# Dilated attention stage of a two-layer encoder: the step without projections between two head groups is taken out

## The chip, the cores and the metric

The kernel runs on one core of a Trainium2 chip. A core has five engines with a queue of instructions each: TensorE (PE, matrix products; its weight loads are listed as PEld), VectorE (DVE), ScalarE (ACT), GpSimd (POOL) and SyncE (SP, which here issues most of the DMAs). An engine takes its queue in order; what it needs of another engine or of a DMA it awaits by semaphore, and everything behind the waiting instruction waits too. Matrix products land in PSUM, of which this stage uses eight banks. The metric is the time of one execution on the device in microseconds (us): the median of the runs.

## What is computed

Two encoder layers over a sequence of 1024 positions with 1024 channels: layer 0 is latent attention, layer 1 is dilated window attention, and each is followed by a squared-ReLU MLP. The change lies in the dilated attention of layer 1, cut here to what matters:

```python
DIL_GROUPS = ((128, 1), (512, 4), (2048, 16))      # (window, dilation)

def dilated_mixer(h, pos, w_in, g_q, g_k, rel_bias, w_o):
    proj = (h @ w_in).reshape(B, S, N_DIL_GROUPS, 3, DIL_HEADS, DIL_HEAD_DIM)
    for gi, (window, dilation) in enumerate(DIL_GROUPS):
        q = rms_norm(proj[:, :, gi, 0], g_q[gi])
        k = rms_norm(proj[:, :, gi, 1], g_k[gi])
        v = proj[:, :, gi, 2]
        o, lse = dilated_group(q, k, v, pos, table, window, dilation)
    wts = jax.nn.softmax(jnp.stack(lses, axis=0), axis=0)
    o = jnp.einsum('gbsh,gbshd->bshd', wts, o_all)
    return o.reshape(B, S, DIL_HEADS * DIL_HEAD_DIM) @ w_o
```

In `dilated_group` the positions are sorted by residue (`_to_residues`), a query sees the keys of its window within its residue, a bias from a table is added, and softmax and the product with v follow. The products are made from float32 split in a high and a low part (three matmuls for one).

## The kernel before

The stage is `dil`. It goes through the three groups one after the other. A group has 16 heads in 8 pairs (`pr`), and a pair takes four steps (`tp` 0 to 3) of two tiles of 128 positions each, so a group has 32 steps. `steps` lists them all. Before the change it has one entry `None` behind each of the first two groups: a step in which PE makes no projections. PE's order is that in which the steps are written (it is pinned from `mark` on); on the other engines a planner places the instructions, so they can stand steps away from where they are written.

One step of the main loop, in PE's order:

- `products` (L1880): score products `pss` of the two tiles that became ready in the step before, from `kT`, six matmuls a tile; a third part of them needs the low half of `kT`, which DVE writes (L1860).
- `project` (L425, L426, L427 in `mm3`): q and k of one tile of 128 positions, 24 matmuls `psproj` from the input tiles `h` in the order d = 0 to 7, each with a high and a low part.
- `stacks` (L1855): four transposes `psq` of the normalized q and k (`qn`) of two steps ago; ACT (L1859) and DVE (L1860) then write `kT`.
- `project` again, for the second tile.
- `av` (L1948, L1949): products of the transposed weights `pT` with v for the tiles whose scores were made in the step before; eight matmuls a tile in the groups 0 and 1, four in group 2. DVE adds the parts up into `U` (L1950).

Beside that `scores` loads the bias `bt` (SP), adds it on DVE (L1894), exponentiates on ACT (L1898, L1900); `attend` splits the weights into `ph` (high part on ACT L1934, low part on DVE or POOL L1935), and a DMA transpose on SP's queue makes `pT` of it (L1936). `qkstep` (L1839 to L1846) normalizes the projections on ACT, DVE and POOL. `v_load` and `v_parts` bring v for two pairs at a time (`vraw` by SP's queue; parts on ACT L1826, DVE L1827, POOL L1828 and L1829). The weights of a pair come as `wqkr` (SP's queue, ACT's for group 2) and are split into `wqkh` on ACT (L121) and `wqkl` on DVE (L122).

The next group needs the same input in another order of positions. `permute(g, dp, k)` copies it: `dp` is a quarter of the channels (d = 2 dp and 2 dp + 1), `k` the high or low part; one call makes two tiles `hTp` by four copies for group 1 and by eight for group 2. The copies go round among the engines: of five, two are on ACT (L2106), two on DVE (L2108), one on POOL (L2110). So there are 32 copies of 128x512 before group 1 and 64 of 128x256 before group 2. The old input has 16 tiles of the pool `gran` with 29 places, and the new needs 16 more, so most of the new tiles take places that something else must leave first. Before the change two of the eight calls are written in the last step of a group and six in the `None` step.

In groups 0 and 1 tile 7 of a pair becomes ready one step later than tiles 5 and 6 (`carry`) and is worked together with tile 0 of the next pair. With the `None` step between, tile 7 of the last pair has an `attend` of its own.

Of the kernel before, what the change touches and what calls it, by code (L numbers as in the profile page):

```python
# [14 lines left out]
AF = mybir.ActivationFunctionType  # L15
ALU = mybir.AluOpType
# [4 lines left out]
P = 128  # L21
# [20 lines left out]
class K:  # L42
# [1717 lines left out]
    def dil(self, at0, at1, tail, wqk, vd):  # L1760
# [147 lines left out]

        def attend(pairs, pe):

            pss = [PS("pss") for _ in range(2)]
            for i, (u, t) in enumerate(pairs):
                products(u, t, pss, i)
            n = len(pairs)
            g = pairs[0][0]["g"]
            m = 4 * P * (1 if g == 2 else 2)
            flat = lambda x: x.rearrange("p i c -> p (i c)")[:, 0 : n * m]
            parts = lambda x: flat(x).rearrange("p (i k c) -> p i k c", i=n, k=2)
            if pe:
                pT = D_("pT", (P, 2, 8 * P), F16, 2)  # L1920
                ps = PS("pspt")
                for i, (u, t) in enumerate(pairs):
                    p = scores(u, t, pss, i)
                    for e in range(2):
                        nc.tensor.transpose(ps[:, (2 * i + e) * P : (2 * i + e + 1) * P], p[:, e], self.ident)
                x = ps[:, 0 : n * 2 * P].rearrange("p (i c) -> p i c", i=n)
                nc.scalar.activation(parts(pT)[:, :, 0], x, AF.Copy)
                nc.vector.tensor_tensor(parts(pT)[:, :, 1], x, parts(pT)[:, :, 0], op=ALU.subtract)
            else:
                ph, pT = (D_(x, (P, 2, 8 * P), F16, 2) for x in ("ph", "pT"))  # L1930
                for i, (u, t) in enumerate(pairs):
                    p = scores(u, t, pss, i)
                    hi, lo = (parts(ph)[:, i, k].rearrange("p (h c) -> p h c", h=2) for k in range(2))
                    nc.scalar.activation(hi, p, AF.Copy)  # L1934
                    (nc.gpsimd if i or g == 2 else nc.vector).tensor_tensor(lo, p, hi, op=ALU.subtract)  # L1935
                nc.sync.dma_start_transpose(out=flat(pT).rearrange("p (b q) -> p b q", q=P), in_=flat(ph))  # L1936
            return [(u, t, parts(pT)[:, i]) for i, (u, t) in enumerate(pairs)]

        def av(u, t, pT):
            g, pr = u["g"], u["pr"]  # L1940
# [115 lines left out]

        steps = []
        for g in range(3):
            steps += [("qk", g, pr, tp) for pr in range(8) for tp in range(4)] + [None] * (1 if g < 2 else 6)
        loads, wts = {}, {}  # L2060
        mark = len(nc.cur_bb.bb.instructions)
        end = max(n for n, x in enumerate(steps) if x is not None)
# [12 lines left out]
        for n, (_, g, pr, _) in firsts.items():  # L2075
            if pr % 2 == 0:
                VS = VSs[(g, pr // 2)] = {}
                VS["load"] = lambda g=g, c=pr // 2, VS=VS: VS.update(raws=v_load(g, c))
                vtodo.setdefault(n - 4, []).append(VS["load"])
                for t in range(0, 9 if g < 2 else 8, 2):  # L2080
                    vtodo.setdefault(n - 2 + t // 2, []).append(lambda t=t, VS=VS: v_parts(VS["raws"], VS, t))
                vtodo.setdefault(n - 2 + t // 2, []).append(lambda VS=VS: VS.pop("raws"))

        h = [at0, at1]
        HT = [at0.tiles, at1.tiles]
# [36 lines left out]
        for n, step in enumerate(steps):  # L2122
            fetch(n + 2)
            for f in vtodo.pop(n, ()):
                f()
            if step is None and perms:
                while perms:
                    permute(*perms.pop(0))
                HT = new
                h = [(lambda k, d, t=t: t[k][d // 2][:, d % 2, :]) for t in HT]  # L2130
            if step is not None and n + 1 < len(steps) and steps[n + 1] is None and step[1] < 2:
                new = [[[], []], [[], []]]
                perms = [(step[1] + 1, dp, k) for dp in range(4) for k in range(2)]
# [226 lines left out]
```

## Time and profile before

| what | value |
| --- | --- |
| median of 3 runs | 3260.46 us (3258.18 to 3262.77) |
| the profiled execution, its own time | 3266.25 us |
| its span | 3264.5 us |
| its granted TensorE clock, mean | 0.982 |
| PE busy | 3145.6 us (96%) |
| dilated stage, first to last projection from `hT` and `hTp` | 1670.9 to 2525.4 us |
| the two places between groups | near 1940 us and 2235 us |

How to read what follows: times are microseconds from the start of the span. A row of the timeline gives start, length, engine, line, what is written and from what, and how many instructions were merged; behind it in brackets, where the engine was idle, how long and what ended the idle time. A row of the view by windows gives the stretch, its length, then for PE, PEld, DVE, ACT and POOL the busy time with the number of instructions, then the granted TensorE clock as a share of full speed, the busy share of the DMA engines, and GB/s. A row of a tile or line gives count and least, median and greatest length in nanoseconds.

### The profile page before, as it was taken

Reading aid. Unit: us, or ns where it says so; the run is one execution under the profiler, and the core shown is the slowest. Engines: PE = TensorE matmul, PEld = TensorE weight load, DVE = VectorE, ACT = ScalarE, POOL = GpSimd, SP = SyncE. Lnnn points to the kernel's source line nnn. Section 1 sums busy time; section 2 is a strip of 40 time slices with the busy share of each in tenths; the row PEclk is TensorE's granted clock in tenths of the full one; section 3 lists DMA queues with packets and bytes.
Section 4 is the critical chain, followed back from the end, with each engine's and each line's share of the span. In section 5 each row is a group of like instructions: output and inputs, shape, how many; then the busy total and the mean of one; then the engine's idle time right before and its main releaser. Section 6 shows DMA issues by size and latency. Waiting matters only on the chain.

```text
span 3264.5 us, 50798 instructions
## 1 busy us (share of the span) xinstructions
PE 3145.6 (96%) x18034; PEld 2660.3 (81%) x18034; DVE 2404.1 (74%) x4272; ACT 1735.4 (53%) x3507; POOL 892.6 (27%) x1197
## 2 busy tenths in 40 slices
PE   6989999999999999999999989998998999999999
PEld 6877677778888788778889989998998788888887
DVE  5677777756977866688767776777888688678566
ACT  5547787754554433542237676666555264444342
POOL 7465555530111000001124444444333002110010
PEclk9999999999999999999999999998999999999999
DMA  5352332252655788535658777887767635439554
GB/s 191 120 188 85 101 95 85 66 188 84 207 184 171 278 228 301 164 126 193 207 142 176 176 176 167 185 181 158 174 153 187 186 104 200 160 138 322 201 192 129
DMA packets 538990, 552.31 MB, mean 169 GB/s; under 512 B 199493, under 2 KB 421106, under 8 KB 538730
## 3 DMA queue, kind: packets, MB, share of 16 engines
q1 hardware_dynamic: 484042, 434.61, 46.8%
q0 software_dynamic: 27360, 91.31, 7.5%
q10 hardware_dynamic: 27328, 23.07, 2.7%
q8 instruction: 144, 2.36, 0.3%
q14 instruction: 116, 0.95, 0.1%
HBM read 376.17 MB, written 132.62 MB: 156 GB/s over the span
## 4 chain that ended last, share of the span: by engine, by line
PE 48%; DVE 5%; DMA 5%; issue 2%; POOL 1%; ACT 1%; SPq 0%; ACTq 0%; DVEq 0%; POOLq 0%
PE psm L426 7%; PE psm L427 7%; PE psm L425 7%; PE psproj L425 4%; PE psproj L426 4%; PE psproj L427 4%; PE pss L1880 2%; DMA pT<-ph 2%; PE psv L426 2%; PE psv L427 2%; PE psv L425 2%; PE psav L1948 1%; PE psy L425 1%; PE psy L427 1%; PE psy L426 1%
## 5 line engine op out<-in xcount | busy, mean ns | idle before, releaser
L426 PE MATMUL psm<-dl,dh 128*128 128x512 f32 x896 | 351.9, 393 | 7.3 <-DVE dl L122 7.2
L425 PE MATMUL psm<-hf,wf 128*128 128x512 f32 x896 | 350.2, 391 | 2.6 <-ACT wf L121 2.6
L427 PE MATMUL psm<-dh,dl 128*128 128x512 f32 x896 | 350.9, 392 | 0.0
L426 PE MATMUL psm<-hf,wf 128*128 128x512 f32 x896 | 349.2, 390 | 0.0
L427 PE MATMUL psm<-hf,wf 128*128 128x512 f32 x896 | 347.3, 390 | 0.4 <-DVE wf L122 0.4
L425 PE MATMUL psm<-dh,dh 128*128 128x512 f32 x896 | 336.5, 393 | 4.9 <-ACT dh L121 4.9
L425 PE MATMUL psproj<-wqkh,hTp 128*128 128x256 f32 x1024 | 307.4, 300 | 0.0
L426 PE MATMUL psproj<-wqkl,hTp 128*128 128x256 f32 x1024 | 294.8, 288 | 0.0
L427 PE MATMUL psproj<-wqkh,hTp 128*128 128x256 f32 x1024 | 294.5, 288 | 0.0
L121 ACT ACTIVATE dh<-ufr 128x1024 fp32r<-128x1024 f32 x112 | 118.3, 1057 | 176.2 <-PE psm L427 52.0
L425 PEld LDWEIGHTS psproj<-wqkh,hTp 128*128 128x128 f32 x1024 | 201.9, 197 | 9.3 <-issue 1.6
L426 PEld LDWEIGHTS psm<-dl,dh 128*128 128x128 f32 x896 | 169.6, 189 | 45.3 <-DVE dl L122 10.1
L425 PEld LDWEIGHTS psm<-dh,dh 128*128 128x128 f32 x896 | 169.0, 189 | 42.3 <-ACT dh L121 7.2
L426 PEld LDWEIGHTS psproj<-wqkl,hTp 128*128 128x128 f32 x1024 | 202.1, 197 | 0.0
L427 PEld LDWEIGHTS psproj<-wqkh,hTp 128*128 128x128 f32 x1024 | 201.3, 197 | 0.0
L425 PEld LDWEIGHTS psm<-hf,wf 128*128 128x128 f32 x896 | 168.6, 188 | 39.8 <-ACT wf L121 5.5
L427 PEld LDWEIGHTS psm<-dh,dl 128*128 128x128 f32 x896 | 169.7, 189 | 35.3
L427 PEld LDWEIGHTS psm<-hf,wf 128*128 128x128 f32 x896 | 168.5, 188 | 36.4 <-DVE wf L122 1.1
L426 PEld LDWEIGHTS psm<-hf,wf 128*128 128x128 f32 x896 | 168.6, 188 | 34.8
L1846 POOL TENSOR_TENSOR qn<-qn,dgain 128x256 f32<-128x256 f32 x96 | 92.1, 959 | 382.1 <-DVE qn L1844 303.0
L122 DVE TENSOR_TENSOR dl<-ufr,dh 128x1024 fp32r<-128x1024 f32 x112 | 136.9, 1222 | 77.2 <-ACT dh L121 58.5
L756 DVE TENSOR_REDUCE mx<-pmx 128x1 f32<-128x512 f32 x256 | 165.1, 682 | 27.5 <-PE pmx L754 27.3
(399 smaller groups left out, 8979.1 us busy)
## 6 DMA issues: line engine op xcount, KB each, us to landing
ufr<-uf SPq DMA_DIRECT2D x112, 512.0 KB
adaw<-in_ada_w SPq DMA_DIRECT2D x96, 512.0 KB
w2r<-in_mlp_w SPq DMA_DIRECT2D x96, 512.0 KB
w1r<-in_mlp_w SPq DMA_DIRECT2D x64, 512.0 KB
bt<-bias SPq DMA_DIRECT2D x128, 256.0 KB
qkv<-st SPq DMA_DIRECT2D x32, 512.0 KB
hraw<-qkv SPq DMA_DIRECT2D x32, 512.0 KB
uf<-ub POOLq DMA_DIRECT2D x32, 512.0 KB, 3.9
```

What stands on the lines that cost most here:

```text
L121: nc.scalar.activation(hi, src, AF.Copy)
L122: (lo_eng or nc.vector).tensor_tensor(lo, src, hi.bitcast(F32), op=ALU.subtract)
L425: mm(out, lh, rh, start=first, stop=False)
L426: mm(out, lh, rl, start=False, stop=False)
L427: mm(out, ll, rh, start=False, stop=last)
L756: nc.vector.tensor_reduce(maxes[h][:, 2 * j + b : 2 * j + b + 1], ps, op=ALU.max, axis=AX.X)
L1846: nc.gpsimd.tensor_tensor(qq, qq, gain[:, g : g + 1, :].unsqueeze(1).broadcast_to([P, 2, 2, 64]), op=ALU.mult)
L1880: nc.tensor.matmul(pss[e][:, i * 256 : (i + 1) * 256], q[r, a, :], u["k"][r, b, w0 : w0 + 256], start=n == 0, stop=n == 2)
L1948: nc.tensor.matmul(o, pT[:, 0, c], v, start=b == 0, stop=False)
```

## The change

The `None` entries behind groups 0 and 1 go; the six at the end of the stage stay. What was written in that step finds other places:

- one `permute` call is written in step `tp` 2 of the group's last pair, two in `tp` 3, and the other five at the head of the next group's first step, ahead of its projections on the other engines' queues;
- tile 7 of a group's last pair is worked with the next group's first tiles: one pair of tiles from two groups between groups 0 and 1, and three tiles together between groups 1 and 2 (group 2 has tiles 0 and 1 ready at once). `attend` therefore takes tiles of different groups and up to three, two score banks for every two tiles; the three fill `ph` and `pT` exactly (2048 columns);
- the first v load of groups 1 and 2 and its parts are written three steps later, counted from the group's first step.

```diff
         def attend(pairs, pe):
-            pss = [PS("pss") for _ in range(2)]
+            pss = []
             for i, (u, t) in enumerate(pairs):
-                products(u, t, pss, i)
-            n = len(pairs)
-            g = pairs[0][0]["g"]
-            m = 4 * P * (1 if g == 2 else 2)
-            flat = lambda x: x.rearrange("p i c -> p (i c)")[:, 0 : n * m]
+                if i % 2 == 0:
+                    pss.append([PS("pss") for _ in range(2)])
+                products(u, t, pss[i // 2], i % 2)
+            m = [4 * P * (1 if u["g"] == 2 else 2) for u, _ in pairs]
+            end = [sum(m[: i + 1]) for i in range(len(m))]
+            flat = lambda x: x.rearrange("p i c -> p (i c)")[:, 0 : end[-1]]
...
-                    (nc.gpsimd if i or g == 2 else nc.vector).tensor_tensor(lo, p, hi, op=ALU.subtract)
+                    (nc.gpsimd if i or u["g"] == 2 else nc.vector).tensor_tensor(lo, p, hi, op=ALU.subtract)
...
-            steps += [("qk", g, pr, tp) for pr in range(8) for tp in range(4)] + [None] * (1 if g < 2 else 6)
+            steps += [("qk", g, pr, tp) for pr in range(8) for tp in range(4)] + [None] * (6 if g == 2 else 0)
...
-                vtodo.setdefault(n - 4, []).append(VS["load"])
+                late = 3 if pr == 0 and g else 0
+                vtodo.setdefault(n - 4 + late, []).append(VS["load"])
                 for t in range(0, 9 if g < 2 else 8, 2):
-                    vtodo.setdefault(n - 2 + t // 2, []).append(lambda t=t, VS=VS: v_parts(VS["raws"], VS, t))
+                    vtodo.setdefault(n - 2 + late + t // 2, []).append(lambda t=t, VS=VS: v_parts(VS["raws"], VS, t))
...
-            if step is None and perms:
+            if step is not None and step[2:] == (0, 0) and perms:
                 while perms:
                     permute(*perms.pop(0))
                 HT = new
                 h = [(lambda k, d, t=t: t[k][d // 2][:, d % 2, :]) for t in HT]
-            if step is not None and n + 1 < len(steps) and steps[n + 1] is None and step[1] < 2:
-                new = [[[], []], [[], []]]
-                perms = [(step[1] + 1, dp, k) for dp in range(4) for k in range(2)]
-                for _ in range(2):
+            if step is not None and step[1] < 2 and step[2] == 7 and step[3] >= 2:
+                if step[3] == 2:
+                    new = [[[], []], [[], []]]
+                    perms = [(step[1] + 1, dp, k) for dp in range(4) for k in range(2)]
+                for _ in range(step[3] - 1):
                     permute(*perms.pop(0))
```

What this makes of PE's order, at the place between groups 0 and 1: before, behind the score products of the `None` step, stand its transposes, its products with v, the next step's score products, and then the first projection from the copied input (`hTp`).

```order
L1880 MATMUL pss_25191<-kT_24580 128x256
L1880 MATMUL pss_25192<-kT_24580 128x256
L1855 MATMUL psq_25230<-ident,qn_24982 128x128 x4
L1948 LDWEIGHTS pT_25024
L1948 MATMUL psav_25237<-vs_24162,pT_25024 128x192
...
L1880 MATMUL pss_25266<-kT_24580 128x256
L1880 MATMUL pss_25267<-kT_24580 128x256
...
L425 MATMUL psproj_25305<-wqkh_25183,hTp_24997 128x256
```

With the change, the same score products are followed at once by the projections of the next group's first step; one of their tiles for d = 2 and 3 (`hTp_25149`) is among those that are copied late.

```order
L1880 MATMUL pss_25181<-kT_24580 128x256
L1880 MATMUL pss_25182<-kT_24580 128x256
L425 MATMUL psproj_25220<-wqkh_25009,hTp_24849 128x256
L426 MATMUL psproj_25220<-wqkl_25010,hTp_24849 128x256
L427 MATMUL psproj_25220<-wqkh_25009,hTp_24997 128x256
...
L425 MATMUL psproj_25220<-wqkh_25009,hTp_25003 128x256
L426 MATMUL psproj_25220<-wqkl_25010,hTp_25003 128x256
L427 MATMUL psproj_25220<-wqkh_25009,hTp_25149 128x256
```

So the transposes, the products with v and one set of score products that stood between two groups' projections now stand behind the next group's first projections.

DVE's queue at the same place, with the change, from the write of `kT` for the next group's first score products to the last copy that the first projection needs (`hTp_25173`, d = 6 and 7, low part). Left out are the four bias additions in the middle, which stand together:

```order
L1860 TENSOR_TENSOR kT_24580<-psq_25083,kT_24580 128x2x256
L122 TENSOR_TENSOR wqkl_25010<-wqkr_24843,wqkh_25009 128x1024
L1953 TENSOR_REDUCE U_24030<-psav_25114 128x128
L1840 TENSOR_REDUCE dms_25135<-dsq_25134 128x8
L1953 TENSOR_REDUCE U_24030<-psav_25124 128x128
L122 TENSOR_TENSOR wqkl_25014<-wqkr_24846,wqkh_25013 128x1024
L2112 CAST hTp_25149<-hTl_20785 128x4x128
L2112 CAST hTp_25155<-hT_3860_18891 128x4x128
L2112 CAST hTp_25158<-hT_3860_18891 128x4x128
...
L2112 CAST hTp_25161<-hsl_19484 128x4x128
...
L2112 CAST hTp_25173<-hT_3880_18987 128x4x128
```

Ten of the 32 copies stand a step or more ahead of this place on their engines; of DVE's 13 copies four do, and the others stand as shown.

On SP's queue three steps ahead of the group's end, before: the v load, then a bias, half of the next weights, and the transpose for the products with v.

```order
L1936 DMA_TRANSPOSE pT_24597<-ph_24596 128x16x128
L1966 DMA U<-U_23473 128x8x128
L1805 DMA vraw_24713<-v 64x256
...
L1810 DMA vraw_24715<-v 64x256
L1889 ISA
L1889 DMA bt_24882<-bias_135 128x2x256
L1562 DMA wqkr_24985<-in_dil_w_in 128x4x128 x2
L1936 DMA_TRANSPOSE pT_24740<-ph_24739 128x16x128
L1562 DMA wqkr_24988<-in_dil_w_in 128x4x128 x2
```

With the change both halves of the weights stand ahead of the v load, and the transpose behind all of it:

```order
L1939 DMA_TRANSPOSE pT_24597<-ph_24596 128x16x128
L1969 DMA U<-U_23473 128x8x128
L1562 DMA wqkr_24843<-in_dil_w_in 128x4x128 x2
L1562 DMA wqkr_24846<-in_dil_w_in 128x4x128 x2
L1889 ISA
L1889 DMA bt_24882<-bias_135 128x2x256
L1805 DMA vraw_24985<-v 64x256
...
L1810 DMA vraw_24987<-v 64x256
L1939 DMA_TRANSPOSE pT_24728<-ph_24727 128x16x128
```

The transpose has moved past two more weight loads of its queue; the v load itself is issued in the same step as before.

More of the change, by code (lines that the diff above doesn't have):

```diff
@@ L1909, in attend @@
         def attend(pairs, pe):
-            pss = [PS("pss") for _ in range(2)]
+            pss = []
             for i, (u, t) in enumerate(pairs):
-                products(u, t, pss, i)
-            n = len(pairs)
-            g = pairs[0][0]["g"]
-            m = 4 * P * (1 if g == 2 else 2)
-            flat = lambda x: x.rearrange("p i c -> p (i c)")[:, 0 : n * m]
-            parts = lambda x: flat(x).rearrange("p (i k c) -> p i k c", i=n, k=2)
+                if i % 2 == 0:
[4 more added lines that the diff above has]
+            flat = lambda x: x.rearrange("p i c -> p (i c)")[:, 0 : end[-1]]
+            parts = lambda x, i: flat(x)[:, end[i] - m[i] : end[i]].rearrange("p (k c) -> p k c", k=2)
             if pe:
@@ L1922, in attend @@
                 for i, (u, t) in enumerate(pairs):
-                    p = scores(u, t, pss, i)
+                    p = scores(u, t, pss[i // 2], i % 2)
                     for e in range(2):
                         nc.tensor.transpose(ps[:, (2 * i + e) * P : (2 * i + e + 1) * P], p[:, e], self.ident)
+                n = len(pairs)
                 x = ps[:, 0 : n * 2 * P].rearrange("p (i c) -> p i c", i=n)
-                nc.scalar.activation(parts(pT)[:, :, 0], x, AF.Copy)
-                nc.vector.tensor_tensor(parts(pT)[:, :, 1], x, parts(pT)[:, :, 0], op=ALU.subtract)
+                y = flat(pT).rearrange("p (i k c) -> p i k c", i=n, k=2)
+                nc.scalar.activation(y[:, :, 0], x, AF.Copy)
+                nc.vector.tensor_tensor(y[:, :, 1], x, y[:, :, 0], op=ALU.subtract)
             else:
@@ L1931, in attend @@
                 for i, (u, t) in enumerate(pairs):
-                    p = scores(u, t, pss, i)
-                    hi, lo = (parts(ph)[:, i, k].rearrange("p (h c) -> p h c", h=2) for k in range(2))
+                    p = scores(u, t, pss[i // 2], i % 2)
+                    hi, lo = (parts(ph, i)[:, k].rearrange("p (h c) -> p h c", h=2) for k in range(2))
                     nc.scalar.activation(hi, p, AF.Copy)
-                    (nc.gpsimd if i or g == 2 else nc.vector).tensor_tensor(lo, p, hi, op=ALU.subtract)
+                    (nc.gpsimd if i or u["g"] == 2 else nc.vector).tensor_tensor(lo, p, hi, op=ALU.subtract)
                 nc.sync.dma_start_transpose(out=flat(pT).rearrange("p (b q) -> p b q", q=P), in_=flat(ph))
-            return [(u, t, parts(pT)[:, i]) for i, (u, t) in enumerate(pairs)]
+            return [(u, t, parts(pT, i)) for i, (u, t) in enumerate(pairs)]
         def av(u, t, pT):
@@ L2078, in dil @@
                 VS["load"] = lambda g=g, c=pr // 2, VS=VS: VS.update(raws=v_load(g, c))
-                vtodo.setdefault(n - 4, []).append(VS["load"])
+                late = 3 if pr == 0 and g else 0
+                vtodo.setdefault(n - 4 + late, []).append(VS["load"])
                 for t in range(0, 9 if g < 2 else 8, 2):
-                    vtodo.setdefault(n - 2 + t // 2, []).append(lambda t=t, VS=VS: v_parts(VS["raws"], VS, t))
-                vtodo.setdefault(n - 2 + t // 2, []).append(lambda VS=VS: VS.pop("raws"))
+                    vtodo.setdefault(n - 2 + late + t // 2, []).append(lambda t=t, VS=VS: v_parts(VS["raws"], VS, t))
+                vtodo.setdefault(n - 2 + late + t // 2, []).append(lambda VS=VS: VS.pop("raws"))
         h = [at0, at1]
```

## The prediction

> **What bounds the kernel now.** I read the page's head first, then the projections by windows, then PE's timeline around the two places between groups, and last DVE's and SP's rows there. Line numbers are those of the kernel before.
>
> ```profile
> span 3264.5 us, 50798 instructions
> PE 3145.6 (96%) x18034; PEld 2660.3 (81%) x18034; DVE 2404.1 (74%) x4272; ACT 1735.4 (53%) x3507; POOL 892.6 (27%) x1197
> 2050.00:2150.00 100.00, 74.13 (x571) 69.51 (x570) 8.28 (x12) 7.09 (x12) 1.00 0.88 196
> 1912.78:1977.32 64.54, 33.45 (x242) 31.71 (x240) 3.46 (x5) 2.91 (x5) 0.84 0.68 167
> 2202.93:2265.41 62.48, 33.79 (x242) 32.05 (x240) 3.46 (x5) 2.96 (x5) 0.84 0.74 157
> ```
>
> PE is the bound nearly everywhere. The three windows count projections only. In a quiet stretch 571 of them fall in 100 us, so a step (48) takes 48 / 5.71 = 8.41 us at full clock. The other two windows run from a transpose `psq` to the one six steps on, the `None` step among them, and hold five steps' projections (242): 64.54 and 62.48 us, where five steps take 42.05. The step without projections also brings work that is not lost: it holds 16 products with v and 6 score products more than five regular steps. A step's work other than projections is 8.41 - 48 x 0.12 = 2.65 us (0.12 is the spacing of two projections, 1936.23 and 1936.35 below); of that I take 0.6, an estimate, 1.6 us. So **lost are 64.54 - 42.05 - 1.6 = 20.9 us at the first place and 18.8 at the second, 39.7 together.** PE's timeline shows where:
>
> ```profile
> 1926.56 0.26 PE L1948 MATMUL psav<-vs,pT 128*128 128x192 bf16 x1 [1.91 <-DMA pT<-ph]
> 1936.23 0.28 PE L426 MATMUL psproj<-wqkl,hsh 128*128 128x256 f32 x1
> 1936.35 0.28 PE L427 MATMUL psproj<-wqkh,hsl 128*128 128x256 f32 x1
> 1938.78 0.74 PE L1880 MATMUL pss<-kT 64*128 64x256 f32 x8 [0.60 <-DVE kT L1860]
> 1944.96 0.34 PE L1948 MATMUL psav<-vs,pT 128*128 128x192 bf16 x1 [4.86 <-DMA pT<-ph]
> 1950.26 1.23 PE L1880 MATMUL pss<-kT 64*128 64x256 f32 x8 [2.26 <-DVE kT L1860]
> 1952.22 0.41 PE L425 MATMUL psproj<-wqkh,hTp 128*128 128x256 f32 x1
> 1961.93 0.34 PE L1948 MATMUL psav<-vs,pT 128*128 128x192 bf16 x1 [2.80 <-DMA pT<-ph]
> ...
> 2218.76 0.34 PE L1948 MATMUL psav<-vs,pT 128*128 128x192 bf16 x1 [3.96 <-DMA pT<-ph]
> 2233.55 0.74 PE L1880 MATMUL pss<-kT 64*128 64x256 f32 x8 [2.37 <-DVE kT L1860]
> 2236.97 0.34 PE L1948 MATMUL psav<-vs,pT 128*128 128x192 bf16 x1 [1.64 <-DMA pT<-ph]
> 2241.74 1.22 PE L1880 MATMUL pss<-kT 64*128 64x256 f32 x8 [1.73 <-DVE kT L1860]
> 2252.70 0.26 PE L1948 MATMUL psav<-vs,pT 128*128 128x192 bf16 x1 [1.20 <-DMA pT<-ph]
> ```
>
> The bracketed waits sum to 12.4 us at the first place and 10.9 at the second. What is left, 8.5 and 7.9, is a slow clock behind each longer wait: projections take 0.41 us instead of 0.28, and the granted clock halves for about 4 us:
>
> ```profile
> 1935.00:1940.00 5.00, 4.40 (x46) 3.76 (x44) 5.00 (x6) 5.00 (x6) 4.33 (x4) 1.00 0.00 0
> 1940.00:1945.00 5.00, 0.14 (x2) 0.04 (x2) 5.00 (x6) 5.00 (x7) 3.49 (x3) 0.91 0.56 105
> 1945.00:1950.00 5.00, 3.00 (x20) 2.40 (x20) 5.00 (x14) 3.08 (x7) 0.00 (x0) 0.50 0.28 71
> 1925.00:1930.00 5.00, 3.44 (x28) 2.94 (x28) 4.17 (x6) 3.15 (x8) 2.68 (x3) 0.70 0.83 252
> ```
>
> Four microseconds at half speed are 2 us lost per drop, and about four drops at each place account for the 8 us. The columns four and five behind the length show DVE and ACT busy for all of 1935 to 1945, POOL for 7.8 of these 10: the engines that copy `hTp` are the bound there, not PE.
>
> **The change part by part.** Call T0 the end of the old group's last projection: 1936.47 (1936.35 + 0.12), and 2229.47 at the second place by the like rows.
>
> *The empty step goes.* PE's later waits at each place (0.60, 4.86, 2.26, 2.80; 2.37, 1.64, 1.73, 1.20) and their slow clock lose their cause, since regular steps stand there. They don't vanish: PE now reaches the first `hTp` projection 2.3 us after T0 (products with v and scores of a regular step, most of the 2.65), and the copies aren't done.
>
> *The copies.* They are as many as before, 32 and 64, at these prices (least, median, greatest, in ns):
>
> ```profile
> L2106 ACT ACTIVATE hTp<-hT x7: 1097/1131/1148, 1919.5 to 1943.5; 128x512 fp32r<-128x512 f32 x7
> L2108 DVE CAST hTp<-hT x6: 598/778/1586, 1923.7 to 1944.9; 128x512 fp32r<-128x512 f32 x6
> L2108 DVE CAST hTp<-hsl x3: 614/1516/1530, 1941.0 to 1945.4; 128x512 fp32r<-128x512 f32 x3
> L2110 POOL TENSOR_SCALAR hTp<-hT x3: 1118/1364/1481, 1916.5 to 1940.6; 128x512 fp32r<-128x512 f32 x3
> L2108 DVE CAST hTp<-hTp x25: 369/398/1355, 2203.7 to 2236.9; 128x256 fp32r<-128x256 f32 x25
> 1938.05 0.68 DVE L1860 TENSOR_TENSOR kT<-psq,kT 128x512 fp32r<-128x512 f32 x1
> 1938.65 2.45 DVE L2108 CAST hTp<-hT 128x512 fp32r<-128x512 f32 x2
> 1945.42 0.61 DVE L2108 CAST hTp<-hsl 128x512 fp32r<-128x512 f32 x1
> 1946.43 0.40 DVE L1894 CUSTOM_DVE_ANT_0 pd<-pss,bt 128x256 f32<-128x256 f32 x1
> 1948.40 1.20 DVE L122 TENSOR_TENSOR wqkl<-wqkr,wqkh 128x1024 fp32r<-128x1024 f32 x1
> 2233.41 3.91 DVE L2108 CAST hTp<-hTp 128x256 fp32r<-128x256 f32 x9
> 2230.80 2.09 DVE L2108 CAST hTp<-hTp 128x256 fp32r<-128x256 f32 x2
> ```
>
> DVE's order at the first place is the one quoted above with the change. The first projection's d = 6 needs the seventh copy of that row of instructions. With lengths less their overlap of about 0.06 (the `kT` row of 0.68 is followed after 0.60) the chain is: `kT` 0.60, split 1.14, two reductions of 0.47 and `dms` 0.60 (rows below), second split 1.14, four bias additions of 0.34, one small operation 0.16, seven copies. Before, the seven copies behind `kT` began at 1938.65 and the last ended at 1946.03, less one reduction of 0.47: 6.9 us.
>
> ```profile
> 1944.41 0.54 DVE L1950 TENSOR_REDUCE U<-psav 128x128 f32<-128x384 f32 x1
> 1929.01 0.68 DVE L1840 TENSOR_REDUCE dms<-dsq 128x8 f32<-128x512 f32 x1
> 1939.07 1.54 POOL L1935 TENSOR_TENSOR ph<-pd,ph 128x512 f16<-128x512 f32 x1
> 1923.15 1.13 SPq L1562 DMA_DIRECT2D wqkr<-in_dil_w_in  x2
> 2208.84 6.16 SPq L1936 DMA_TRANSPOSE pT<-ph  x1
> ```
>
> Sum 0.60 + 1.14 + 0.94 + 0.60 + 1.14 + 1.36 + 0.16 + 6.9 = 12.8. If `kT` and the first split are done when the first products with v land (T0 + 0.6), the other 11.1 end at T0 + 11.7; if DVE starts the chain only then, at T0 + 13.4. I take T0 + 12.5. Then follow four matmuls (0.5), the second projection (24 x 0.12 = 2.9) and one drop of the clock (2), 5.4 in all, where a regular step ends at T0 + 8.4: **loss 9.5 at the first place**. Bounds: with seven copies at 0.55 from T0 + 11.7, 5.6; with all at 1.5 from T0 + 13.4, 14.0.
>
> At the second place the row of instructions has, behind `kT` and the splits, 15 copies, two reductions, `dms` and two bias additions. Alone a copy takes 3.91 / 9 = 0.43, beside POOL's 2.09 / 2 = 1.05; I take 0.5, nearer to the long row. From T0 + 0.5: 7.5 + 1.54 + 0.56 makes T0 + 10.1, and **the loss is 10.1 + 5.4 - 8.4 = 7.1** (bounds 6.1 and 15.4 by the two prices). ACT needs about as long but its last needed copy, 1.13 each, stands no later; taken as inside these bounds.
>
> *SP's queue and the v load.* At the first place the transpose now stands behind two more weight loads: their issue is 1.13, and their 0.5 MB at the 252 GB/s of the window 1925 to 1930 take 2.1, so 3.2 us if all is exposed, 0 if the transfers were done. The early waits of 1.91 and 3.96, each with a drop of the clock of 2, belong to the steps ahead of the empty one and stay as I forecast it: **3.9 and 6.0**; bounds 0 (the load comes at another moment and the wait is gone) to 7.1 at the first, 2.0 to 8.0 at the second. The parts of v (three engines, 0.6 to 1.2 each) move into steps in which PE is busy throughout and DVE 74% of the span; cover is that step, so 0, and if it is gone some 0.6 each on DVE at the first place.
>
> *Tiles of two groups in one `attend`.* The score products are as many, in other steps; the one transpose for three tiles carries the same 16 blocks as a regular one. Cost 0, hidden by nothing, because nothing is added; bounds 0 to 2 for a step with 18 products in a row.
>
> **Sum.** Lost after: 9.5 + 3.9 + 7.1 + 6.0 = 26.5, against 39.7: **13.2 us less**. The profiled execution took 3266.25 us and has a span of 3264.5; with the change 3253.1 and 3251.3. The median of the runs is 3260.46, 5.8 below that execution, so the forecast is **3247.3 us**. All low bounds together lose 5.6 + 6.1 + 0 + 2 = 13.7 (3234.5), all high ones 14.0 + 15.4 + 7.1 + 8.0 = 44.5 (3265.3).
>
> [...]
>
> [...]
>
> **The rivals.** *Everything is hidden:* the copies run early enough and the early waits are gone too. For it speaks that POOL is busy for 27% of the span only; against it that DVE and ACT are full for the ten microseconds around T0. Lost would be about the low bounds, 13.7, or less: 3232 to 3235.
>
> *The wait only changes its place:* DVE and ACT have the same work between the groups, and with both at 5.00 of 5 us, PE waits as long as before, now within the projection. The lost time then stays at 39.7 but for the one or two drops of the clock that fewer waits make: 3258 or so. Against it: the chain that counted before went through copies, exponentials, `ph`, the transpose and back to PE, and only its first part counts now.
>
> *Slower: all copies go at the long price, and the transposed weights come late behind them.* DVE and POOL then copy side by side throughout. At 1.5 and 1.05 us a copy the gate costs 14.0 and 15.4, with the early 9.9 as much as is lost now: 39.3. The next group's scores are made before its projections, but their exponentials and bias additions stand behind the last copies. From there it is an addition and an exponential (some 2.4 by neighbouring rows, an estimate), `ph` 1.5 (the row at 1939.07), and the transpose: 4.35 from that row's end, 1940.61, to the products at 1944.96, or 9.9 from the issue at 2208.84 to the products at 2218.76. So `pT` is there 8.3 to 13.8 after the last copy, and PE needs it one regular step after the delayed one, 5.4 + 8.4 = 13.8 after that copy. In the forecast this is never late; it decides where the transpose takes its 9.9 and the exponentials wait two more microseconds for ACT's own copies (two of 1.13): 2 late and a drop of 2 at each place, lost 39.3 + 8 = 47.3, or 3260.5 + 7.6 = 3268.
>
> **How the numbers follow.** A measurement of this kernel tells about 0.2% (6.5 us) from no change, so faster means under 3253.9 and slower over 3267. Chances: forecast 0.56 (own range 3241 to 3254), hidden 0.10, changed place 0.15, slower 0.19, of which a quarter stays within 0.2%. Faster holds nearly all of the forecast (0.55) and all of hidden: 0.65. The same: the changed place, the forecast's end and that quarter, 0.21. Slower: 0.14. The range 3235 to 3264 leaves out about half of the hidden and three quarters of the slower case.
>
> **What would show it.** In the changed kernel's trace the waits for `pT` of 4.86, 2.80 and 1.64 and those for `kT` of 2.26 and 1.73 are gone; one wait or a row of short ones stands inside `psproj` from `hTp`, ended by DVE (or ACT) at the copies' line, 10.2 us long at the first place (T0 + 12.5 less T0 + 2.3) less some 2 of projections that run meanwhile, so about 8, and 6 at the second. The window of five steps shrinks from 64.54 to 42.05 + 13.4 = 55.5 and from 62.48 to 55.2. The early waits for `pT`, near 1926 and 2218, remain. I am wrong on the size if copies take above 1.2 us on DVE, on the mechanism if PE's longest wait there is again for `pT`, and on the early terms if these waits are gone.

## The result and the profile after

The changed kernel takes as long as the one before: 3264.22 us (median of 14 runs) against 3261.73 (14 runs), a ratio of 1.0008 with an interval of 0.9996 to 1.0021, or -1 to +7 us. Forecast were 13 us less (3247.3).

The page of the changed kernel, span and first line of busy times: the work is the same, and PE is again busy for 96%.

```profile
span 3268.5 us, 50788 instructions
...
PE 3143.2 (96%) x18034; PEld 2659.3 (81%) x18034; DVE 2395.8 (73%) x4271; ACT 1732.8 (53%) x3507; POOL 893.3 (27%) x1198
```

The projections by windows in the changed kernel, each window from the `psq` that corresponds to the first of the window shown of before, over the same five steps (stretch, length, PE, PEld, DVE, ACT, granted clock, DMA share, GB/s):

```profile
1917.92:1973.16 55.24, 34.43 (x242) 31.94 (x240) 3.46 (x5) 2.96 (x5) 0.91 0.74 176
2201.15:2260.21 59.06, 34.32 (x242) 31.75 (x240) 3.82 (x6) 2.94 (x5) 0.88 0.77 156
```

The first was forecast at 55.5 us and is 55.24; the second at 55.2, and is 59.06. PE's timeline of the changed kernel, its longer waits, and the old group's last projection (the row without a wait):

```profile
1932.84 0.26 PE L1951 MATMUL psav<-vs,pT 128*128 128x192 bf16 x1 [3.05 <-DMA pT<-ph]
...
1942.60 0.28 PE L427 MATMUL psproj<-wqkh,hsl 128*128 128x256 f32 x1
...
1949.78 0.38 PE L425 MATMUL psproj<-wqkh,hTp 128*128 128x256 f32 x1 [3.06 <-DVE hTp L2112]
...
1953.88 0.58 PE L427 MATMUL psproj<-wqkh,hTp 128*128 128x256 f32 x1 [2.88 <-DVE hTp L2112]
...
2229.20 0.39 PE L425 MATMUL psproj<-wqkh,hTp 128*128 128x256 f32 x1 [0.92 <-ACT hTp L2110]
...
2234.31 0.58 PE L427 MATMUL psproj<-wqkh,hTp 128*128 128x256 f32 x1 [4.60 <-DVE hTp L2112]
...
2252.46 0.34 PE L1951 MATMUL psav<-vs,pT 128*128 128x192 bf16 x1 [4.04 <-DMA pT<-ph]
...
2283.34 0.26 PE L1951 MATMUL psav<-vs,pT 128*128 128x192 bf16 x1 [2.48 <-DMA pT<-ph]
...
2328.65 0.26 PE L1951 MATMUL psav<-vs,pT 128*128 128x192 bf16 x1 [1.89 <-DMA pT<-ph]
...
2535.24 1.65 PE L1880 MATMUL pss<-kT 64*128 64x256 f32 x11 [7.24 <-DVE qn L1844]
```

The waits of the empty step are gone, and those for copies (3.06, 2.88; 0.92, 4.60) stand within the first projections, as forecast. New are four further down: 4.04, 2.48 and 1.89 for transposed weights, and 7.24 at the stage's end, where before waited 0.59 and 3.93 us.

To add this up, I read the start of each step's first projection from PE's timeline and number the steps in the order in which these starts show, from 0. (The first two of the program don't show apart, so group 0 ends with step 29, group 1 with 61. Where the expectations speak of group 2's fifth step, it is 66; what they call its eleventh or twelfth is 71, in e11 70 and 71.) The stage's parts in us, in the first and second profile of each kernel; "end" is from the start of step 93 to the first product behind the stage:

```
                          steps 24-36    59-66       67-92         end
before                    131.0 129.2   86.6 86.1   232.9 229.1   13.46 13.46
changed                   125.5 124.9   87.3 86.5   235.2 236.7   16.15 16.18
difference of the means      -4.9         +0.6         +4.9         +2.7
forecast                     -7.5         -5.7          0            0
```

The differences sum to +3.3 us, near the runs' +2.5; the forecast is -13.2. So the first place gave two thirds of what was forecast, the second nothing, and group 2 and the stage's end lost what the first gave. The last column agrees to 0.03 us between the two profiles of a kernel; 67 to 92 scatters by 1 to 4 us between profiles of one kernel, so its +4.9 is the least certain of the four.

### The profile page after: what moved, and what is told of

It is laid out like the page before. It is cut to its first block, busy times and chain, and to the rows that moved or that the text cites. A ratio compares the mean times of both kernels' runs of the same rounds, so it can differ in the third digit from the quotient of the medians.

```text
span 3268.5 us, 50788 instructions
## 1 busy us (share of the span) xinstructions
PE 3143.2 (96%) x18034; PEld 2659.3 (81%) x18034; DVE 2395.8 (73%) x4271; ACT 1732.8 (53%) x3507; POOL 893.3 (27%) x1198
## 4 chain that ended last, share of the span: by engine, by line
PE 48%; DVE 5%; DMA 4%; issue 2%; ACT 2%; POOL 1%; SPq 0%; DVEq 0%; ACTq 0%; POOLq 0%
PE psm L426 7%; PE psm L427 7%; PE psm L425 7%; PE psproj L425 4%; PE psproj L427 4%; PE psproj L426 4%; PE pss L1880 2%; DMA pT<-ph 2%; PE psv L426 2%; PE psv L427 2%; PE psv L425 2%; PE psav L1951 1%; PE psy L425 1%; PE psy L426 1%; PE psy L427 1%
```

## The experiments

Three theories at the start: A, the second place alone gains nothing; B, both places gain and the time is lost behind them; C, what is lost behind them is scatter between runs. All kernels start from the changed one, but where the text says otherwise. Each ratio is against runs of the kernel before that were taken beside it; the median of these goes from 3259.57 to 3265.14 us, so medians from different experiments are not compared with each other.

**One place at a time.** In `e1_first_only` only the first empty step goes, in `e2_second_only` only the second.

```diff
-            steps += [...] + [None] * (6 if g == 2 else 0)
+            steps += [...] + [None] * (6 if g == 2 else 1 if g == 1 else 0)      # e1; g == 0 in e2
```

> The step without projections is taken out between groups 0 and 1 only; between groups 1 and 2 all is as before. Theory A (the first place gained about 5.6 us from step 24 to step 37, the second nothing): 4 to 7 us less than before, and the first projections of steps 24 to 37 stand as in the changed kernel within 1 us. Theory B (both places gain, and the time is lost in group 2 and in the stage's end by the other order there): 6 to 9 us less, since group 2 and the end stand as before. Theory C (only the scatter of single runs): any lead that this profile shows at the first place differs by 3 us or more from the changed kernel's.

> The step without projections is taken out between groups 1 and 2 only. Theory A: no gain, -1 to +2 us against before; the wait for copies (4.6 in the changed kernel) and the wait for pT one step later (4.0) are there again. Theory B: gain of some 5 us at the place itself, lost again behind it: waits for pT near the sixth and the twelfth step of group 2, and 7 us instead of 4 at the stage's end. Theory C: those later waits are as in the kernel before.

e1: 3260.52 us against 3265.14, ratio 0.9993 (0.9981 to 1.0004), a smaller gain than either theory had. e2: 3270.14, ratio 1.0017 (1.0006 to 1.0027): the second edit alone makes the kernel slower by some 0.2%. By the parts: e1 has 125.5, 85.5, 232.9 and 16.77; e2 129.5, 83.1, 235.4 and 16.76. So e2 gains 3 us at its place, loses them again in steps 67 to 92 (235.4 against 229.1 and 232.9 of before; step 71 takes 12.00, step 72 10.09, where before has 7.85 and 8.4), and 3.3 more at the end. That is against A. For B, the waits at 2280.20 and 2325.51 in e2 are those of the changed kernel; only e1's end, which B expected as before, is as long as e2's.

**Second profiles.** `e4_same_again` and `r5_before_again`.

> The changed kernel once more, for a second profile. Theories A and B: the waits of 3 us at the first place, 4.6 and 4.0 at the second, 2.5 and 1.9 in group 2 and 7 at the stage's end come again within 0.5 us. Theory C: those in group 2 and at the end differ by 1 us or more.

> The kernel before once more, for a second profile. The end of the stage waits 0.6 and 3.9 us in the first profile of before and 6.5 to 7.3 in all four kernels with the change or a part of it. If that difference belongs to the change: 4 to 5 us again. If it is scatter between runs: 6 to 7. And the steps behind the second place: without the change the twelfth step of group 2 should be at 7.9 us again, not 11 to 12.

The changed kernel's waits come again: 3.06 and 2.88 at the first place, 4.66 and 3.66 at the second, 2.15 and 1.14 in group 2 (2.48 and 1.89 in the first profile), 7.28 at the end (one run 3266.68 us). Before has 0.58 and 3.93 at the end again, and step 71 at 7.84 (one run 3258.25). C falls.

**v in its old steps.** `e3_v_not_late`, and `e6_first_only_v`, which is e1 with this edit. The old steps are counted from the new group's first one. Against the old group's steps the first load of group 1 then comes two steps earlier than in the kernel before: it begins in step 25 in e3, in step 27 in before and in the changed kernel.

```diff
-                late = 3 if pr == 0 and g else 0
+                late = 0
```

> The changed kernel, but with the first v load of groups 1 and 2 and its parts in their old steps. If the late load of v is what delays pT in group 2 (wait of 2.48 at 2283): that wait is gone, 2 to 4 us less than the changed kernel. If it is the weights' load and the order of SP's queue: the same waits, and at the two places the v parts lie beside the copies, 1 to 3 us more.

> The empty step taken out at the first place only, v in its old steps. By the profiles of e1 and e3 the first place gives 9 us in place of 5.5 and the second is as before: 5 to 9 us less than before, ratio 0.9975 to 0.9985. If the late v is not the cause of the early wait for pT at the first place, it is as e1: 2 us less.

e3: 3259.55 us, ratio 0.9983 (0.9972 to 0.9993); that is 8 us under the changed kernel's ratio. The wait of 2.25 in step 66 stays, so v is not its cause; but the early wait of 3.05 at the first place is gone. SP's timeline of the changed kernel there, and of e3:

```profile
1925.77 0.60 SPq L1810 DMA_DIRECT2D vraw<-v  x1
1926.69 3.91 SPq L1939 DMA_TRANSPOSE pT<-ph  x1
```

```profile
1916.14 1.02 SPq L1889 DMA_DIRECT2D bt<-bias  x2
1920.69 1.80 SPq L1939 DMA_TRANSPOSE pT<-ph  x1
```

With v late, seven of its loads stand directly ahead of the transpose, whose issue takes 3.91 us, and PE gets `pT` 6.2 us after it began. Without them the issue takes 1.80, PE doesn't wait, and step 28 goes from 12.2 and 12.8 to 8.41. e6 has 122.1 us in steps 24 to 36, 8 less than before, and 16.77 at the end; measured 3259.67, ratio 0.9992 (0.9983 to 1.0001), less than was expected and no better than e1's 0.9993.

**Without the copies.** `e5_no_copies` leaves out the copies of the input; the groups 1 and 2 project it in its old order.

```diff
-                    permute(*perms.pop(0))
-                HT = new
...
+                    perms.pop(0)
```

> Leaves out the copies of the input: the groups 1 and 2 project the input in the old order of positions. Otherwise the changed kernel with v in its old steps. If the copies alone set what is lost at the places: steps 28 to 31 and 59 to 66 at 8.4 to 8.8 us each, the stage 20 to 26 us shorter than in that kernel (6 to 10 from the first place, 10 to 14 from the second, where the late pT goes with them). If the transposes behind the weights' load are a cause of their own: the wait of 3 for pT in the step after the scores of group 2's first tiles stays at 2 us or more.

One run, 3237.07 us; the parts are 112.9 and 75.4, so the copies cost e3 10.9 us at the first place and 11.6 at the second. But step 63 still takes 13.38. From e5's timelines of PE, SP and ACT:

```profile
2224.29 0.34 PE L1951 MATMUL psav<-vs,pT 128*128 128x192 bf16 x1 [3.12 <-DMA pT<-ph]
```

```profile
2207.27 1.81 SPq L1939 DMA_TRANSPOSE pT<-ph  x1
...
2213.71 3.94 SPq L1939 DMA_TRANSPOSE pT<-ph  x1
```

```profile
2212.82 0.94 ACTq L1562 DMA_DIRECT2D wqkr<-in_dil_w_in  x2
```

The transpose of 2207.27 is used at 2212.62 with no wait, so it takes 5.4 us at most. That of 2213.71 is begun 0.9 us after ACT's queue starts on the next pair's weights (four loads, 1 MB), and takes until 2224.29, 10.6 us. No copy is in this kernel, so the late `pT` is a cause of its own. The changed kernel shows the same:

```profile
2240.05 1.49 ACTq L1562 DMA_DIRECT2D wqkr<-in_dil_w_in  x3
```

```profile
2241.87 4.36 SPq L1939 DMA_TRANSPOSE pT<-ph  x1
```

From 2241.87 to 2252.46 are again 10.6 us; in e2, e3 and e7 it is 7.8 to 8.5. The kernel before had it too: its transpose of 2208.84 took 9.9. The last of the four weight loads there, from ACT's timeline of before (four v loads of SP's queue, from 2201.47 on, stand ahead as well):

```profile
2207.47 0.37 ACTq L1562 DMA_DIRECT2D wqkr<-in_dil_w_in  x1
```

**The weights behind the transpose.** `e8_weights_later` writes that load one step later; `e9_weights_held`, whose edit is shown, writes it in its old step but keeps it, on ACT's queue, behind the ACT instructions that are written before it. Both have v in its old steps.

```diff
+            if firsts.get(n + 2, (0, 0, 0, 0))[1:3] == (2, 1):
+                self.held(lambda: fetch(n + 2))
+            else:
                 fetch(n + 2)
```

> The changed kernel with v in its old steps, and the weights of group 2's second pair loaded one step later on ACT's queue. If the transpose is late since 1 MB of weights is loaded ahead of it: the wait of 3.0 for pT one step after the copies falls under 1 us and that step from 12.2 to 9.5 or less. If the transpose is late for another reason (its scores are late): 2.5 to 3.5 again.

> The changed kernel with v in its old steps, and the load of the weights of group 2's second pair (1 MB on ACT's queue) kept behind the weights ph of the next attend, so that it no longer stands ahead of the transpose. If the transpose takes 10.6 us instead of 4 to 5 because it queues with these weights: the wait of 3.0 for pT behind the copies falls under 1, that step from 12.2 to 9.5 or less, the eight steps of the second place from 87 to 82 to 84. If the transpose is slow or late for another reason: 2.5 to 3.5 again and 86 to 87.

e8 did not test it: in its program the weights stand at their old place on ACT's queue, and step 63 still waits 2.95. What moved is the next v load, ahead of two transposes. e9 did. Its ACT timeline, SP's and PE's:

```profile
2238.69 0.62 ACT L1937 ACTIVATE ph<-pd 128x512 f16<-128x512 f32 x1
...
2244.78 2.05 ACTq L1562 DMA_DIRECT2D wqkr<-in_dil_w_in  x4
```

```profile
2235.55 2.86 SPq L1939 DMA_TRANSPOSE pT<-ph  x1
```

```profile
2241.36 0.26 PE L1951 MATMUL psav<-vs,pT 128*128 128x192 bf16 x1 [0.96 <-DMA pT<-ph]
```

With no weights ahead of it the transpose takes 5.8 us in place of e3's 7.8, the wait is 0.96, step 63 takes 9.52 and the second place 81.5. This does not rest on one profile. In e3, e7, e8 and `e8_timed` the weights stand ahead, and this transpose begins 1.61 us into step 63 and takes 7.4 to 8.0; in e9 and the three kernels below that hold the weights back too (e10 to e12) it begins 1.60 us into the step and takes 5.7 to 5.9. Over all e9 gains nothing on e3 by the ratios (3255.51, ratio 0.9988, 0.9979 to 0.9998; e3 0.9983): step 66 still takes 10.20 and step 71 12.13.

**The statistics on SP's queue.** Behind the last `finish` of group 1 SP writes the softmax statistics S and reads them back in the new order. SP's timeline of the changed kernel:

```profile
2269.19 2.71 SPq L1815 DMA_DIRECT2D vraw<-v  x4
2272.01 0.55 SPq L1981 DMA_DIRECT2D S<-stat  x1
2276.39 1.20 SPq L1988 DMA_DIRECT2D stat<-S  x2
2277.76 3.30 SPq L1939 DMA_TRANSPOSE pT<-ph  x1
```

The read waits 3.7 us, till 2276.39, for the write, and the transpose stands behind it; PE waits 2.48 for it. In the kernel before, a transpose stands between the write and the read:

```profile
2264.98 0.53 SPq L1978 DMA_DIRECT2D S<-stat  x1
2266.47 1.24 SPq L1936 DMA_TRANSPOSE pT<-ph  x1
2268.14 1.25 SPq L1985 DMA_DIRECT2D stat<-S  x2
```

`e7_s_on_pool` gives the reads to POOL's queue (v in its old steps).

```diff
-                        nc.sync.dma_start(out=stat[64 * i : 64 * i + 64, k]...
+                        nc.gpsimd.dma_start(out=stat[64 * i : 64 * i + 64, k]...
```

> The changed kernel with v in its old steps; the two reads of the statistics S go through POOL's queue instead of SP's. If the wait of 2.2 to 2.5 for pT in the fifth step of group 2 comes from the transpose standing behind these reads on SP (they wait for the write of S): it is gone, that step at 8.4 to 9 instead of 10.8. If not: 10.4 to 11 again.

SP's timeline of e7:

```profile
2262.98 0.55 SPq L1981 DMA_DIRECT2D S<-stat  x1
2264.82 2.89 SPq L1939 DMA_TRANSPOSE pT<-ph  x1
```

The transpose now follows the write by 1.8 us, not 5.8, and step 66 takes 8.42. Step 71 takes 7.86 (one run, 3251.48 us).

**Versions.** `e8_timed` is e8 again; `e10_held_v_earlier` is e9 with the v load for group 2's third and fourth pair one step earlier; `e11_both` is e9 and e7 together.

> The kernel of e8_weights_later again, with timing. In its program the weights did not move on ACT's queue ahead of the transpose, but the v load for the third and fourth pair moved ahead of two transposes and of the statistics. By its profile (3252.1 us span) 6 to 10 us under before, and the fifth step of group 2 again at 8.4; if that profile was scatter, no better than e3 (5.5 under before).

> As e9, and the v load for group 2's third and fourth pair one step earlier, so that it is through before the statistics and the transposes behind them. If SP's queue around the statistics causes the wait in the fifth step of group 2 and those of 1.1 and 0.9 six steps later: both go, as in e8, and the time is 8 to 14 us under before. If these are scatter: no better than e9 by more than 2 us.

> e9 and e7 together: v in its old steps, the weights of group 2's second pair behind ph, the reads of the statistics on POOL's queue. Theory (weights ahead of the transpose, and the statistics' reads ahead of the next): the eight steps of the second place at 79 to 82 us (e9 81.5, less the 2.4 of its fifth step), the eleventh and twelfth step of group 2 at 10.2 and 7.9 as in e7, 8 to 12 us under before. If the late step of 12.1 (in e9) has a cause of its own: it stays at 11 to 12.

e8_timed: 3252.14 us, ratio 0.9976 (0.9967 to 0.9986); step 66 at 8.41 and step 71 at 7.85 as in e8's first profile, with the reads still on SP's queue; so moving the v load ahead of the statistics cures step 66 as well. e10: 3252.19, ratio 0.9983 (0.9974 to 0.9992), no better than e8 and, by the intervals, not clearly better than e9; its step 66 takes 9.69. e11: 3252.84 against 3261.35, **ratio 0.9967 (0.9953 to 0.9980), 11 us under before**, the lowest, though the interval overlaps that of `e8_timed`. Its second place takes 81.6 and step 71 7.86, which e9 has at 12.13, but step 66 still 9.48, and steps 67 to 92 together 234.9, no less than in the changed kernel.

**Step 71.** It does not follow from step 66: e5, e9 and e10 have step 66 at 10.2, 10.2 and 9.7, and step 71 at 7.85, 12.13 and 7.85. Over all sixteen profiles it goes with the order of two queues in step 70. ACT's and SP's timelines of the changed kernel, then of before:

```profile
2318.08 0.60 ACT L1839 ACTIVATE dsq<-psproj 128x512 f32<-128x512 f32 x1
2318.96 0.38 ACTq L1562 DMA_DIRECT2D wqkr<-in_dil_w_in  x1
2320.20 1.35 SPq L1939 DMA_TRANSPOSE pT<-ph  x1
```

```profile
2320.60 0.60 ACT L1839 ACTIVATE dsq<-psproj 128x512 f32<-128x512 f32 x1 [1.44 <-PE psproj L427]
2321.24 1.23 SPq L1936 DMA_TRANSPOSE pT<-ph  x1
2321.48 0.39 ACTq L1562 DMA_DIRECT2D wqkr<-in_dil_w_in  x1
```

In five profiles (both of the changed kernel, e2, e3, e9) the next pair's weights begin 1.2 us ahead of this transpose, and step 71 takes 11.0 to 12.1 us. In the other eleven they begin 0.2 to 1.4 us behind it, and step 71 takes 7.85. ACT comes to the weights when PE has made step 70's projections, and there lies the difference: PE waits 1.9 to 2.4 us for `kT` in step 69 in all sixteen, but in the five step 70 then takes 8.7 us and none of its projections is slow; in the eleven it takes 9.6 to 10.9, and 6 to 21 of them take some 0.41 us in place of 0.28. The granted clock (the figure third from the end) of before and of the changed kernel, same windows:

```profile
2310.00:2315.00 5.00, 3.16 (x21) 3.03 (x22) 5.00 (x7) 2.74 (x12) 4.92 (x5) 0.77 0.02 5
2310.00:2315.00 5.00, 4.19 (x39) 4.06 (x39) 5.00 (x15) 2.63 (x10) 4.05 (x4) 1.00 0.02 5
```

So where PE keeps its clock it is some 1.5 us earlier, the weights go ahead of the transpose, and PE waits 1.1 to 2.0 us for `pT`: steps 69 to 72 take 39.2 to 41.2 us in the five, 36.8 to 38.8 in the eleven. This is read from the profiles. No run sets that order alone; how much the weights slow this transpose is not shown (in the eleven it is used 7.8 to 9.1 us after its issue without a wait, in the five after 7.7 to 8.6); and why the clock stays up in the five is open.

**The stage's end.** Of each kernel's program I looked up what the last two score products wait for: the PSUM places they get were last used by other tiles, and which ones depends on how many tiles, and in what order, were asked for since the stage's start. The changed kernel asks for two score tiles fewer. e1 does so too and e2 asks for as many as before, and yet both get other places, so the order counts as well as the number. PE's timeline of before, of e1 and of `e12_places`, which is e11 with the places turned by four:

```diff
+            if step is not None and step[1:] == (1, 3, 1):
+                for _ in range(4):
+                    nc.vector.memset(PS("pad")[:, 0:1], 0.0)
```

> e11 with four one-column writes of zeros to four more places of PSUM in the middle of group 1, which nothing reads. They only turn the order in which places are handed out. Theory (the stage's end is longer by the place that the last score products get): in this program the first of them gets the place of the very last projections, so that it waits for their normalization, and the end takes 18 to 18.5 us in place of 16.2. If the end is longer for another reason: 16 again.

```profile
2531.32 1.65 PE L1880 MATMUL pss<-kT 64*128 64x256 f32 x11 [3.93 <-DVE U L1950]
```

```profile
2526.43 1.65 PE L1880 MATMUL pss<-kT 64*128 64x256 f32 x12 [7.11 <-DVE qn L1844]
2529.09 0.76 PE L425 MATMUL psy<-woh,oT 128*128 128x512 f32 x1 [1.00 <-issue]
```

```profile
2518.00 1.65 PE L1880 MATMUL pss<-kT 64*128 64x256 f32 x12 [10.40 <-DVE qn L1844]
```

In before the scores get a place of the last products with v and wait for their sum `U`; in the changed kernel one of the last step but one's projections, which is free only when `qn` is made of it; in e1 that and, for the first product behind the stage, the place of the very last projections; in e12 these for the scores themselves. The end takes 13.46, 16.15, 16.77 and 18.99 us in this order; e12, 2.8 above e11's 16.23, was expected at 18 to 18.5 (one run, 3252.61, in which the longer end is lost among the scatter of the other steps).

## Why the prediction was wrong

- **What bounds the kernel, and the first place: right.** The copies' last wait was forecast to end at T0 + 12.5; T0 is 1942.72 here, it ends at 1953.88, so T0 + 11.2. Steps 29 and 30 lose 0.9 + 8.5 = 9.4 us against 8.41, forecast 9.5. The early term was forecast at 3.9; step 28 loses 3.8 and 4.4. Not forecast are losses of 1.0 in step 36 and of 1 to 2 in steps 24 to 27, which make 4.9 of the gain of 7.5. What the early term is, I had put down to two weight loads, with v's load only in the low bound ("the load comes at another moment and the wait is gone"); e3 shows that it is v's load.
- **The second gate: right in mechanism.** The copies' last wait ends at T0 + 11.0 (T0 is 2223.34), forecast 10.1; step 62 loses 8.1, forecast 7.1. The early term of 6.0 was too high: steps 59 and 60 lose 2.1.
- **The step that failed is the arrival of `pT` behind the second gate.** The third rival puts it 8.3 to 13.8 us after the last copy (3.9 until the transpose begins, 4.35 to 9.9 for the transpose) and PE there after 13.8, so that in the forecast it "is never late". PE came as forecast: it was ready for `pT` at 2248.42 (2252.46 less the wait of 4.04), 14.1 us after the copies' wait ended at 2234.31. But `pT` came 18.2 after it: the transpose began after 7.6 us, not 3.9, and took 10.6. By estimates from these rows it took both: begun after 3.9, a transpose of 10.6 would have been 0.4 us late, and begun after 7.6, one of 5.8 (e9's) 0.7 early. The price is high without copies too (10.6 in e5), because the regular order brings the next pair's weights directly ahead of the transpose; e9 takes them away. Steps 63 and 64 lose 7.2 us; in e3 they lose 5.0, and in e9, without the weights ahead, 1.5. I had the row for this, the transpose of 2208.84 that took 9.9, and used it as an upper bound of something that I did not look up: what else was on the DMA queues at that moment.
- **The sum stopped at the end of the second window.** Without the empty step the read of the statistics falls ahead of a transpose: step 66 loses 3.2 us (e7, with the reads on another queue, has 8.42). Steps 69 to 72 lose 2 to 4 us with the weights ahead of a transpose once more, which was seen in the profiles and not tested.
- **"Cost 0, because nothing is added" was wrong for `attend`.** The products are as many, but two PSUM tiles fewer change the places of all that come after, and the stage's end pays 2.7 us, shown by the releasers and by e12.
- The late v, costed at 0 to 3 us, costs about 8 by the ratios of e3 and the changed kernel (5.5 below and 2.6 above before; each is uncertain by 3 to 4), but nothing by those of e6 and e1 (0.9992 and 0.9993). The profiles show 1.4 (e3) and 3.4 (e6 against e1) at the first place. What it costs in all was not settled.
- Of the rivals, "the wait only changes its place" (3258, 2.5 us less) and "slower" (3268, 7.6 more) lie about equally far from the 2.5 us more that were measured. The first is wrong in its reason: the copies' wait is shorter than what it replaced, and the rest was lost elsewhere. The second named the right wait, `pT` late behind the copies at the second place, but hung it on slow copies, and those were near the forecast.
- One reading is misnamed: in the rows by windows DVE and ACT are the third and fourth figures behind the length, not the fourth and fifth. The values taken are theirs.

## What to carry to other kernels

When a step is taken out of a loop, the other queues' order shifts against the main engine by that step: for each transfer that is waited for behind the place, list what now stands ahead of it on every DMA queue, not on its own alone, until the old order is met again (here a transpose took 7.4 to 8.0 us where 1 MB of weights stood ahead of it on another queue, 5.7 to 5.9 where they did not). The tiles asked of a rotating pool are part of the order too: in e1, with two fewer at the first place, the stage's end sixty steps on took 16.77 us, in before 13.46. And a row that is far from its like (a transpose of 9.9 us beside one of 4.35) should be explained before it serves as a bound.

## What the runs showed that was not expected

- A DMA transpose of 16 blocks took 4.3 us from its issue to its use where PE waited for it in the kernel before (issued at 1940.63, 1957.62 and 2232.67), 5.7 to 5.9 in e9 to e12, 6.2 to 7.2 behind seven v loads on its own queue (first place, changed kernel in both profiles and e1), and 7.4 to 10.6 in eight profiles where 1 MB of loads had begun on ACT's queue 0.9 to 3.5 us before (10.6 in the changed kernel and in e5). So loads on another queue delay the transpose here: 7.8 us in e3, 5.8 in e9, which holds these loads back. In what way they delay it, no row shows.
- The clock did not fall behind every wait. The windows of the changed kernel (length, PE, PEld, DVE, ACT, POOL, granted clock, DMA share, GB/s):

```profile
1945.00:1950.00 5.00, 1.94 (x13) 1.62 (x14) 5.00 (x8) 5.00 (x8) 2.54 (x2) 1.00 0.26 48
1950.00:1955.00 5.00, 2.12 (x13) 1.92 (x13) 4.93 (x18) 5.00 (x12) 1.21 (x1) 0.63 0.37 108
```

  In windows of 1 us, the wait of 3.06 up to 1949.78 left it at 1.00 until 1951; it was 0.63 from 1951 to 1952, with the next wait, of 2.88, just begun, and 0.50 from 1952 to 1958. In the kernel before, a wait of 1.91 up to 1926.56 was followed by 0.50 from 1927 to 1930. In step 69 a wait of 2.25 up to 2311.84 was followed by 0.50 from 2313 to 2316 in the kernel before, and one of 2.33 up to 2310.81 by 1.00 in the changed kernel. So in these rows the length of one gap alone does not decide it.
